# A decoder layer on one core: feed-forwards in blocks of eight width tiles with sums in DRAM, memory keys and values first

## The chip, the core and the metric

One core of a Trainium2 chip runs the whole program. Its engines work side by side and wait for each other by semaphores: PE (TensorE, products), DVE (VectorE), ACT (ScalarE), POOL (GpSimd) and SP (SyncE, which here issues loads). PEld is PE's weight load, which overlaps its products. The metric is the device time of one execution, in microseconds.

## The reference, cut to what matters

All arrays are float32. x is 256 x 2048, mem is 256 x 2048, the width of a feed-forward is 5504 = 43 tiles of 128.

```python
h = swiglu(rms_norm(x, ffn1_pre), ffn1_wg, ffn1_wu, ffn1_wd)   # (silu(u @ wg) * (u @ wu)) @ wd
x = x + 0.5 * rms_norm(h, ffn1_post)
m = hybrid_mixer(rms_norm(x, mix_pre), mem, ...)
x = x + rms_norm(m, mix_post)
h = swiglu(rms_norm(x, ffn2_pre), ffn2_wg, ffn2_wu, ffn2_wd)
x = x + 0.5 * rms_norm(h, ffn2_post)
```

The mixer projects u with w_in (5894 columns) into three branches: a gated linear recurrence (six heads, written hgrn), an attention with a forget gate (six heads, fox) and an attention over the memory (four heads), whose keys and values are rms_norm(mem) @ w_mem_kv (1024 columns). Each branch goes through its own output matrix, is multiplied with a sigmoid gate (u @ w_gate, 6144 columns) and added; w_o closes the mixer.

## The kernel before, in words

**Products.** Every large product goes through `linear` (L249). Its left side lies transposed in SBUF, 128 rows of the contraction (a k tile) by 128 tokens; there are two token tiles t. Both sides are kept as two halves, hi (rounded to the float32r format) and lo (what is left), and one product is three matmuls: hi x hi (L278), hi x lo (L279), lo x hi (L281). The right side comes in column chunks of up to 512, mostly two at a time. `linear` walks k in batches: `head` k tiles first, then two at a time, `tail` last, and in each batch token tile 0 then 1. With `by_chunk` the last batch goes chunk by chunk. `evac` takes the sums out of PSUM and may return a step to be done one batch later (transposes, mostly). `before(k)` is called ahead of a batch, `ahead()` once all weights are asked for.

**Weights** (class at L186). `load` (L204) takes a `raw` tile of 2048 columns, so 1 MB (two k tiles of 1024 columns) per DMA on SP's queue (L217); there are three raw tiles. `split` (L162) makes hi on ACT (L164) and lo on DVE (L165) into rings of N_SPLIT = 6 tiles, one k tile of 1024 columns each. With `early`, the first k tiles go to work tiles instead. The first product of feed-forward 1 loads 512 KB at a time (kb=1).

**Buffers.** 21 work tiles (`slot`, 4 KB per partition), 7 temporaries (`tmp`, 2 KB), 3 raw tiles, PSUM as 5 banks for sums (`acc`) and 3 for transposes (`tp`). The transposed, split input u of a sub-layer has its own tiles (`new_uT`). The order of instructions on each engine is fixed ahead of the run by the framework's scheduler, which takes the program's order as priority and lets a later instruction pass where an earlier one isn't ready; so the constants of L544 to L546 are loaded at the very start.

**Stages.**
1. `before_first` (L484): during the first gate product of feed-forward 1, each chunk of x (128 x 512) is loaded on SP's queue (L464), transposed on PE (L171), multiplied with the gain per row and split (L182 on ACT, L183 on DVE), and its squares are summed (L160 on ACT). The norm's row factor r isn't applied to u: it is given as `scale` when sums leave PSUM (L391, L396).
2. `ffn` (L378): the width goes in three parts, PARTS = (0, 16), (16, 32), (32, 43). In each part gate and up products of 8 width tiles alternate (the last 3 tiles in one product), then the down product over the part, in two halves of 1024 columns. The sums of part 1 are copied to y tiles in SBUF by ACT (L438), part 2 is added by DVE (L440), part 3 is added in the closing step.
3. `closer` (L311): `chunk` adds, sums squares and multiplies with the gain row; `post(t)` makes the row factor (`rsqrt`, L129), adds the residual (L360), stores x (L367) and makes the next sub-layer's transposed input. `begin` issues the gain and residual loads on POOL's queue (L308, L327).
4. During the last down product of feed-forward 1 (`before_close`) and in `before_kv`, memory is prepared as x was. The K/V product follows feed-forward 1 and lies between it and the mixer.
5. Mixer: `proj` products in the order mq, hgrn half 0, hgrn half 1, fox. The recurrences and attentions are generators in `tasks`; `step` runs one step of the first two tasks after each batch of a product.
6. Gates and branches, then w_o with a closing step, whose last batch is BIG = 6 k tiles; the first two weight tiles of feed-forward 2 are split early (`first2`, `ahead`), and its first batch is BIG as well. Then feed-forward 2 and the output, stored by SP (L362).

Of the kernel before, what the change touches and what calls it, by code (L numbers as in the profile page):

```python
# [17 lines left out]
P = 128  # L18
# [35 lines left out]
def layer(ctx: ExitStack, tc: tile.TileContext, a, out: bass.AP):  # L54
# [22 lines left out]

    def acc(w):
        return psp.tile([P, 512], F32, tag="acc", bufs=N_ACC, name=nm("acc"))[:, :w]

    def tp(*shape):
        n = int(np.prod(shape))
        t = psp.tile([P, 512], F32, tag="tp", bufs=N_TP, name=nm("tp"))[:, :n]
        if len(shape) == 2:
            t = t.rearrange("p (a b) -> p a b", b=shape[1])
        return t
# [12 lines left out]
    def columns(rows, q):  # L99
        """Vectors [1, n * 128] as n columns each, found by col()."""  # L100
# [16 lines left out]
    turn_first = columns([("ffn1_pre", 16)], S)  # L117
    turn_rest = columns([("mem_norm", 16), ("mix_pre", 16), ("ffn2_pre", 16), ("hgrn_lb", 12), ("hgrn_gnorm", 6)], G)
# [55 lines left out]
    def split_T(hi, lo, src, n, gain=None):  # L174
        """hi, lo: [P, n, 128] slices for src^T (times gain per row)."""
# [10 lines left out]
    class Weights:  # L186
# [3 lines left out]
        def __init__(self, nk, chunks, kb=None, early=0):  # L190
# [6 lines left out]
            self.kb = kb or max(1, 2048 // self.width)  # L197
# [6 lines left out]
        def load(self, n):  # L204
            width, k0 = self.width, len(self.parts)
            raw = pool.tile([P, 2048], F32, tag="raw", bufs=N_RAW, name=nm("raw"))[:, :n * width]
            raw = raw.rearrange("p (k c) -> p k c", c=width)
# [11 lines left out]
            kh = max(1, 1024 // width)  # L219
            for j in range(0, n, kh):  # L220
                m = min(kh, n - j)
                if k0 + j < self.early:
                    hi, lo = slot([P, 1024], F32R, "ehi"), slot([P, 1024], F32R, "elo")
                else:
                    hi = pool.tile([P, 1024], F32R, tag="whi", bufs=N_SPLIT, name=nm("whi"))
                    lo = pool.tile([P, 1024], F32R, tag="wlo", bufs=N_SPLIT, name=nm("wlo"))
                hi = hi[:, :m * width].rearrange("p (k c) -> p k c", c=width)
                lo = lo[:, :m * width].rearrange("p (k c) -> p k c", c=width)
                split(hi, lo, raw[:, j:j + m, :])
                for i in range(m):  # L230
                    self.parts.append((hi[:, i, :], lo[:, i, :]))
# [717 lines left out]
```

## Time and profile before

| | us |
|---|---|
| median of 3 runs | 2263.7 (2262.32 to 2264.56) |
| span of the profiled execution, first to last instruction | 2262.2 |
| PE busy | 2243.5 |
| DVE busy | 1245.6 |
| ACT busy | 1048.0 |
| POOL busy | 33.1 |

The profile gives the profiled execution's span alone; the runs' times hold also what lies around it. Busy time is the union of an engine's instructions, without those that issue, wait or branch. DMAs moved 434.33 MB, 192 GB/s over the span. The clock granted to PE was 0.998 of full speed in the mean.

### The profile page before, as it was taken

Reading aid. Unit: us, or ns where it says so; the run is one execution under the profiler, and the core shown is the slowest. Engines: PE = TensorE matmul, PEld = TensorE weight load, DVE = VectorE, ACT = ScalarE, POOL = GpSimd, SP = SyncE. Lnnn points to the kernel's source line nnn. Section 1 sums busy time; section 2 is a strip of 40 time slices with the busy share of each in tenths; the row PEclk is TensorE's granted clock in tenths of the full one; section 3 lists DMA queues with packets and bytes.
Section 4 is the critical chain, followed back from the end, with each engine's and each line's share of the span. In section 5 each row is a group of like instructions: output and inputs, shape, how many; then the busy total and the mean of one; then the engine's idle time right before and its main releaser. Section 6 shows DMA issues by size and latency. Waiting matters only on the chain.

```text
span 2262.2 us, 26732 instructions
## 1 busy us (share of the span) xinstructions
PE 2243.5 (99%) x10674; PEld 1914.7 (85%) x10674; DVE 1245.6 (55%) x1519; ACT 1048.0 (46%) x1351; POOL 33.1 (1%) x61
## 2 busy tenths in 40 slices
PE   9999999999999999999999999999999999999998
PEld 7888888888898799999888888888888888888896
DVE  5545445454456856686555545557545445455455
ACT  6444444443446744445444444446444444443443
POOL 0000000000000000000000000000000000000000
PEclk9999999999999999999999999999999999999999
DMA  8555565557555644546656566665656555557553
GB/s 267 187 191 189 178 206 187 201 172 258 188 182 197 224 154 154 166 151 176 194 179 199 187 197 216 217 208 188 203 187 186 187 202 186 186 192 255 179 184 121
DMA packets 138540, 434.33 MB, mean 192 GB/s; under 512 B 9080, under 2 KB 42064, under 8 KB 138416
## 3 DMA queue, kind: packets, MB, share of 16 engines
q1 hardware_dynamic: 133568, 417.41, 55.6%
q0 software_dynamic: 4672, 15.15, 2.4%
q8 instruction: 83, 1.36, 0.2%
q14 instruction: 41, 0.34, 0.0%
q10 hardware_dynamic: 176, 0.07, 0.0%
HBM read 426.30 MB, written 6.30 MB: 191 GB/s over the span
## 4 chain that ended last, share of the span: by engine, by line
PE 97%; DMA 1%; DVE 1%; ACT 0%; SPq 0%; issue 0%; DVEq 0%; ACTq 0%
PE acc L278 31%; PE acc L279 31%; PE acc L281 31%; PE tp L171 2%; PE tp L671 1%; DMA x<-in_x_dram 0%; DMA raw<-in_ffn_wu_dram 0%; DMA x<-in_mem_dram 0%; DVE y L360 0%; DVE wlo L165 0%; ACT whi L164 0%; PE tp L584 0%; PE tp L600 0%; ACT junk L160 0%; PE tp L665 0%; PE tp L818 0%
## 5 line engine op out<-in xcount | busy, mean ns | idle before, releaser
L165 DVE TENSOR_TENSOR wlo<-raw,whi 128x1024 fp32r<-128x1024 f32 (+2 forms) x818 | 958.5, 1177 | 866.0 <-ACT whi L164 829.1
L164 ACT ACTIVATE whi<-raw 128x1024 fp32r<-128x1024 f32 (+2 forms) x818 | 833.2, 1024 | 1006.6 <-PE acc L281 956.4
L278 PE MATMUL acc<-whi,uh 128*128 128x512 f32 (+1 forms) x2264 | 856.6, 379 | 1.6 <-ACT uh L182 1.5
L279 PE MATMUL acc<-wlo,uh 128*128 128x512 f32 (+1 forms) x2264 | 849.2, 376 | 0.8 <-DVE wlo L165 0.8
L281 PE MATMUL acc<-whi,ul 128*128 128x512 f32 (+1 forms) x2264 | 670.2, 376 | 0.1
L278 PEld LDWEIGHTS acc<-whi,uh 128*128 128x128 f32 x2264 | 425.0, 188 | 68.2 <-ACT uh L182 3.0
L279 PEld LDWEIGHTS acc<-wlo,uh 128*128 128x128 f32 x2264 | 425.2, 188 | 66.5 <-DVE wlo L165 1.3
L281 PEld LDWEIGHTS acc<-whi,ul 128*128 128x128 f32 x2264 | 421.1, 188 | 66.6 <-DVE ul L183 0.5
L278 PE MATMUL acc<-whi,hh 128*128 128x512 f32 x688 | 269.2, 391 | 0.0
L279 PE MATMUL acc<-wlo,hh 128*128 128x512 f32 x688 | 268.0, 390 | 0.0
L281 PE MATMUL acc<-whi,hl 128*128 128x512 f32 x688 | 228.4, 389 | 0.0
L281 PEld LDWEIGHTS acc<-whi,hl 128*128 128x128 f32 x688 | 129.1, 188 | 26.9
L278 PEld LDWEIGHTS acc<-whi,hh 128*128 128x128 f32 x688 | 129.2, 188 | 26.5
L279 PEld LDWEIGHTS acc<-wlo,hh 128*128 128x128 f32 x688 | 129.2, 188 | 26.3
L396 DVE SCALAR_TENSOR_TENSOR sg<-acc,rstd,sg 128x512 f32<-128x512 f32 (+1 forms) x44 | 31.2, 733 | 34.3 <-PE acc L281 29.9
L278 PE MATMUL acc<-whi,eh 128*128 128x512 f32 x128 | 50.1, 391 | 0.0
L279 PE MATMUL acc<-wlo,eh 128*128 128x512 f32 x128 | 49.8, 389 | 0.0
L391 ACT ACTIVATE sg<-acc,rstd 128x512 f32<-128x512 f32 (+1 forms) x44 | 27.7, 677 | 44.0 <-PE acc L281 43.3
L281 PE MATMUL acc<-whi,el 128*128 128x512 f32 x128 | 42.9, 391 | 0.0
L183 DVE SCALAR_TENSOR_TENSOR ul<-tp,vec,uh 128x128 fp32r<-128x128 f32 x96 | 29.6, 345 | 7.3 <-ACT uh L182 7.0
L182 ACT ACTIVATE uh<-tp,vec 128x128 fp32r<-128x128 f32 x96 | 31.1, 380 | 5.5 <-DVE ul L183 4.2
L281 PEld LDWEIGHTS acc<-whi,el 128*128 128x128 f32 x128 | 24.0, 188 | 5.0
(262 smaller groups left out, 1097.1 us busy)
## 6 DMA issues: line engine op xcount, KB each, us to landing
raw<-in_ffn_wd_dram SPq DMA_DIRECT2D x84, 1024.0 KB, 5.4
raw<-in_ffn_wu_dram SPq DMA_DIRECT2D x80, 1024.0 KB, 4.9
raw<-in_ffn_wg_dram SPq DMA_DIRECT2D x72, 1024.0 KB, 4.9
raw<-in_w_gate_dram SPq DMA_DIRECT2D x48, 1024.0 KB, 5.2
raw<-in_w_in_dram SPq DMA_DIRECT2D x96, 384.0 KB, 3.7
raw<-in_w_o_dram SPq DMA_DIRECT2D x16, 1024.0 KB, 5.6
raw<-in_ffn_wg_dram SPq DMA_DIRECT2D x16, 512.0 KB, 4.7
raw<-in_w_mem_kv_dram SPq DMA_DIRECT2D x8, 1024.0 KB, 5.0
```

The source lines that it names most:

```text
L164: S.activation(hi, src, AF.Copy)
L165: V.tensor_tensor(lo, src, f32(hi), ALU.subtract)
L171: PE.transpose(p[:, i, :], src[:, i * P:(i + 1) * P], ident)
L182: S.activation(hi[:, i, :], p[:, i, :], AF.Copy, scale=g)
L183: V.scalar_tensor_tensor(lo[:, i, :], p[:, i, :], g, f32(hi[:, i, :]), ALU.mult, ALU.subtract)
L278: PE.matmul(ps[t][c], lh, wh[:, sl], start=(k == 0), stop=False)
L279: PE.matmul(ps[t][c], lh, wl[:, sl], start=False, stop=False)
L281: PE.matmul(ps[t][c], ll, wh[:, span[c]], start=False, stop=(k == nk - 1))
L391: S.activation(sg[t][:, i * 512:i * 512 + p.shape[-1]], p, AF.Silu, scale=r(t))
L396: V.scalar_tensor_tensor(h, p, r(t), h, ALU.mult, ALU.mult)
L671: PE.matmul(L[:, 2 * i + j, :], K[:, i, j * P:(j + 1) * P], Q[:, i, j * 64:(j + 1) * 64], start=True, stop=True)
```

## The change

Sizes: N_SLOT 21 to 28 (the u tiles now come from these), N_TMP 7 to 5, N_RAW 3 of 2048 columns to 8 of 1024, one pool of 8 PSUM banks for `acc` and `tp`. Order: the K/V product is the program's first; in it memory is prepared at k = 0, 4, 8, 12, and x is loaded by POOL (two tiles of 512 KB per token tile, at k = 4 and 10), its rows are summed and multiplied with their row factor (6, 12), transposed and split (8, 14), so that feed-forward 1 needs no row factor. Feed-forwards: after the gate product of each block of 8 width tiles the down product of the block before, whose sums leave PSUM through ACT and are stored or added in DRAM by a DMA of POOL's queue; the last down product (11 width tiles) closes, with the sums loaded back. Closing steps after the first keep the residual times a power of two per row. The first mixer product is hgrn's and has a first batch of BIG; mq follows it.

```diff
-N_SLOT = 21
-N_TMP = 7
-N_RAW = 3
+N_SLOT = 28
+N_TMP = 5
+N_RAW = 8
-N_ACC = 5
-N_TP = 3
+N_BANK = 8
+BLOCK = 8
...
 class Weights:
-            self.kb = kb or max(1, 2048 // self.width)
+            self.kb = max(1, 1024 // self.width)
...
     def new_uT():
...
+        return [[(slot([P, 8, P], F32R, "uh"), slot([P, 8, P], F32R, "ul")) for _ in range(2)] for _ in range(2)]
...
     def closer(y, gpost, factor, resid, keep, gname, final, ms=None, unscale=None):
         def begin(half):
+            if ms is not None:
+                j = slot([P, 1024], F32, "junk")
+                S.activation(j, gp[half], AF.Square, accum_out=g2[:, half:half + 1])
...
+                for t in range(2):
+                    k = scales[t][0] if ms is not None else unscale[t] if unscale is not None else None
+                    if k is not None:
+                        for x in xr[t]:
+                            S.activation(x, x, AF.Copy, scale=k)
...
     def ffn(u, r, first, head, wg, wu, wd, gpost, resid, keep, gname, final, unscale=None):
+        ysum = dram.tile([T, D], F32, name=nm("ysum"))
...
+        def down(f0, f1, close=None):
...
+                    x = tmp([P, 512], "part")
+                    S.activation(x, ps, AF.Copy)
+                    dst = ysum[t * P:(t + 1) * P, c * 512:(c + 1) * 512]
+                    if f0 == 0:
+                        G.dma_start(out=dst, in_=x)
+                    else:
+                        G.dma_start(out=dst, in_=x, accum_op=ALU.add)
...
+                       tail=BIG if close and half else 4, by_chunk=by_chunk)
+        last = n_tile // BLOCK * BLOCK
+        for f in range(0, last, BLOCK):
+            if f == 0:
+                linear(lu, first, gate_plain, head=head)
+            else:
+                linear(lu, Weights(KD, chunks(wg, f, BLOCK)), gate_plain)
+                down(f - BLOCK, f)
+            linear(lu, Weights(KD, chunks(wu, f, BLOCK)), lambda t, ps, f=f: up(t, ps, f, BLOCK))
...
+        def start(half):
+            for t in range(2):
+                G.dma_start(out=y[t][half], in_=ysum[t * P:(t + 1) * P, half * 1024:(half + 1) * 1024])
+            begin(half)
+
+        down(last - BLOCK, n_tile, (start, chunk, post))
...
+    def before_kv(k):
...
+        t = 0 if k < 10 else 1
+        if k in (4, 10):
+            xs[t] = [slot([P, 1024], F32, "xs") for _ in range(2)]
+            for h in range(2):
+                G.dma_start(out=xs[t][h], in_=x_in[t * P:(t + 1) * P, h * 1024:(h + 1) * 1024])
+        if k in (6, 12):
...
+            for c in range(4):
+                sumsq(xs[t][c // 2][:, (c % 2) * 512:(c % 2) * 512 + 512], s_x[t][:, c:c + 1])
+            r = pre_rstd(s_x[t])
+            for h in range(2):
+                S.activation(xs[t][h], xs[t][h], AF.Copy, scale=r)
+        if k in (8, 14):
+            for c in range(4):
+                split_T(*uT_part(u0, t, c), xs[t][c // 2][:, (c % 2) * 512:(c % 2) * 512 + 512], 4, col("ffn1_pre", 4 * c, 4))
...
-           Weights(KD, [(W["w_mem_kv"], 0, 512), (W["w_mem_kv"], 512, 512)]), evac_kv, before=before_kv)
+           Weights(KD, [(W["w_mem_kv"], 0, 512), (W["w_mem_kv"], 512, 512)]), evac_kv, before=before_kv, tail=2)
+    first = Weights(KD, [(W["ffn1_wg"], 0, 512), (W["ffn1_wg"], 512, 512)])
+    u1, st1, sq1 = ffn(u0, None, first, 2, W["ffn1_wg"], W["ffn1_wu"], W["ffn1_wd"], a["ffn1_post"], x_in, x1,
+                       "mix_pre", None)
...
-        proj([(c0, W3), (768 + c0, W3)], evac_qf)
+        proj([(c0, W3), (768 + c0, W3)], evac_qf, head=2 if half else BIG)
...
+    tasks.append(hgrn(0, *hgrn_in(0)))
     proj([(5382, 512)], evac_mq)
     tasks.append(mem_attention())
-    tasks.append(hgrn(0, *hgrn_in(0)))
```

## Rows read from the trace of the kernel before

**Rows 1.** The page, part 1: busy us, share of the span, instructions, by engine.
```profile
PE 2243.5 (99%) x10674; PEld 1914.7 (85%) x10674; DVE 1245.6 (55%) x1519; ACT 1048.0 (46%) x1351; POOL 33.1 (1%) x61
```
**Rows 2.** Stretches: us, busy PE, PEld, DVE, ACT, POOL (instructions), PEclk, DMA share, GB/s.
```profile
0.00:60.00 60.00, 54.50 (x246) 43.64 (x247) 35.45 (x69) 40.86 (x77) 4.48 (x12) 1.00 0.76 252
10.00:20.00 10.00, 9.08 (x42) 7.45 (x42) 7.26 (x12) 7.83 (x17) 0.00 (x0) 1.00 0.87 289
...
730.00:760.00 30.00, 30.00 (x147) 24.60 (x146) 28.93 (x65) 25.48 (x60) 4.34 (x8) 1.00 0.66 229
760.00:790.00 30.00, 28.40 (x135) 23.09 (x135) 22.51 (x65) 21.58 (x46) 0.00 (x0) 1.00 0.60 192
...
950.00:1000.00 50.00, 50.00 (x319) 49.78 (x318) 41.50 (x70) 22.17 (x33) 0.00 (x0) 1.00 0.44 143
...
1490.00:1570.00 80.00, 79.97 (x368) 65.83 (x367) 56.50 (x101) 48.88 (x95) 4.34 (x8) 1.00 0.62 211
...
2245.00:2262.20 17.20, 6.16 (x28) 4.76 (x26) 10.58 (x21) 3.39 (x8) 3.49 (x2) 0.78 0.33 122
```
**Rows 3.** Waits of PE: us in total, times, longest.
```profile
PE tp L171 <- DMA x<-in_x_dram: 1.8, 3, 0.9
PE tp L171 <- DMA x<-in_mem_dram: 1.6, 1, 1.6
...
PE acc L279 <- DVE wlo L165: 0.8, 1, 0.8
```
**Rows 4.** The chain in order of time: start, us, what; transposes of feed-forward 1.
```profile
103.17 0.87 PE tp L171 x8
...
192.03 0.87 PE tp L171 x8
```
**Rows 5.** Groups by line: count, busy us, mean ns, idle before.
```profile
L440 DVE TENSOR_TENSOR y<-acc,y 128x512 f32<-128x512 f32 x16 | 11.0, 690 | 17.8 <-PE acc L281 17.8
...
L438 ACT ACTIVATE y<-acc 128x512 f32<-128x512 f32 x16 | 9.5, 592 | 23.6 <-PE acc L281 23.6
```
**Rows 6.** DMA issues: count, KB each, median us from issue to landing.
```profile
raw<-in_ffn_wg_dram SPq DMA_DIRECT2D x72, 1024.0 KB, 4.9
...
raw<-in_ffn_wg_dram SPq DMA_DIRECT2D x16, 512.0 KB, 4.7
...
x<-in_x_dram SPq DMA_DIRECT2D x8, 256.0 KB, 5.3
```
**Rows 7.** The chain in order of time, its first 50 us: two DMAs.
```profile
2.60 8.42 DMA x<-in_x_dram
...
38.81 7.40 DMA raw<-in_ffn_wu_dram
```
**Rows 8.** Timeline of the start: start us, us, engine, line, operation.
```profile
3.91 0.59 POOL L544 DMA_DIRECT2D causal<-in_c_causal_dram  x1
...
7.42 0.73 PE L278 MATMUL acc<-whi,uh 128*128 128x512 f32 x2 [0.46 <-ACT uh L182]
```
**Rows 9.** ACT's groups by line in the first 60 us.
```profile
L164 ACT ACTIVATE whi<-raw 128x1024 fp32r<-128x1024 f32 x21 | 22.0, 1058 | 11.4 <-DMA raw<-in_ffn_wg_dram 5.9 <-DMA raw<-in_ffn_wu_dram 3.4 <-PE acc L281 1.0
L182 ACT ACTIVATE uh<-tp,vec 128x128 fp32r<-128x128 f32 x32 | 10.3, 360 | 4.3 <-DVE ul L183 3.0 <-PE tp L171 1.3
L160 ACT ACTIVATE junk<-x 128x512 f32<-128x512 f32 x8 | 5.0, 625 | 0.3 <-DMA x<-in_x_dram 0.3
```
**Rows 10.** Timeline of PE, then of DVE, from mixer to feed-forward 2.
```profile
1536.74 0.39 PE L278 MATMUL acc<-ehi,uh 128*128 128x512 f32 x1
...
1549.04 0.47 PE L278 MATMUL acc<-ehi,uh 128*128 128x512 f32 x1
...
1545.32 1.21 DVE L165 TENSOR_TENSOR wlo<-raw,whi 128x1024 fp32r<-128x1024 f32 x1
```
**Rows 11.** Timeline of PE in a mixer product of two chunks of 384.
```profile
868.46 0.33 PE L278 MATMUL acc<-whi,uh 128*128 128x384 f32 x1
...
869.50 0.33 PE L278 MATMUL acc<-whi,uh 128*128 128x384 f32 x1
```

More of the change, by code (lines that the diff above doesn't have):

```diff
@@ L205, in load @@
             width, k0 = self.width, len(self.parts)
-            raw = pool.tile([P, 2048], F32, tag="raw", bufs=N_RAW, name=nm("raw"))[:, :n * width]
-            raw = raw.rearrange("p (k c) -> p k c", c=width)
+            raw = raw_tile()[:, :n * width].rearrange("p (k c) -> p k c", c=width)
             off = 0
@@ L218, in load @@
                 off += w
[L219 to L231, printed above, removed]
+            if k0 < self.early:
+                hi, lo = slot([P, 1024], F32R, "ehi"), slot([P, 1024], F32R, "elo")
+            else:
+                hi, lo = split_tiles()
+            hi = hi[:, :n * width].rearrange("p (k c) -> p k c", c=width)
+            lo = lo[:, :n * width].rearrange("p (k c) -> p k c", c=width)
+            split(hi, lo, raw)
+            for i in range(n):
+                self.parts.append((hi[:, i, :], lo[:, i, :]))
     soon = []
@@ new lines, in post, with ffn, scale, chunks @@
+                q = rsqrt(s3, D) if ms is None else rsqrt(s3, D, 1, scales[t][1])
+                rstd[t] = keep_small()
+                V.tensor_copy(rstd[t], q)
+                V.tensor_scalar(s3, s3, 1.0 / D, None, ALU.mult)
+                square[t] = s3
+        square = {}
+        return begin, chunk, post, lambda: u, rstd, square, scales
+    def ffn(u, r, first, head, wg, wu, wd, gpost, resid, keep, gname, final, unscale=None):
+        hT = {}
+        sg = {}
+        n_tile = DFF // P
+        lu = from_uT(u)
+        ysum = dram.tile([T, D], F32, name=nm("ysum"))
+        if r is not None:
+            minus = [keep_small() for _ in range(2)]
+            for t in range(2):
+                V.tensor_scalar(minus[t], r[t], -1.0, None, ALU.mult)
+        def scale(t, sign=1):
+            return float(sign) if r is None else r[t] if sign > 0 else minus[t]
+        def chunks(W, f, n):
+            return [(W, c * P, min(512, (f + n - c) * P)) for c in range(f, f + n, 4)]
+        def gate_plain(t, ps):
+            sg[t] = slot([P, 1024], F32, "sg")
+            for i, p in enumerate(ps):
+                S.activation(sg[t][:, i * 512:i * 512 + p.shape[-1]], p, AF.Silu, scale=scale(t))
+        def up(t, ps, f, n):
+            g = sg[t]
+            for i, p in enumerate(ps):
+                h = g[:, i * 512:i * 512 + p.shape[-1]]
+                V.scalar_tensor_tensor(h, p, scale(t), h, ALU.mult, ALU.mult)
+            def later():
+                for i in range(0, n, 4):
+                    m = min(4, n - i)
+                    if t == 0:
+                        hT[f + i] = (slot([P, 4, 2, P], F32R, "hh"), slot([P, 4, 2, P], F32R, "hl"))
+                    hh, hl = hT[f + i]
+                    split_T(hh[:, :m, t, :], hl[:, :m, t, :], g[:, i * P:(i + m) * P], m)
+            return later
+        def down(f0, f1, close=None):
@@ L442, in evac2 @@
[L442 to L446 removed]
+                    if close:
+                        close[1](t, c, ps, True)
+                        return
+                    x = tmp([P, 512], "part")
[3 more added lines that the diff above has]
+                        G.dma_start(out=dst, in_=x)
+                    else:
+                        G.dma_start(out=dst, in_=x, accum_op=ALU.add)
@@ L447, in ffn, with evac @@
+                def evac(t, ps, half=half):
+                    if close and half == 1:
+                        close[2](t)
                 rows = wd[f0 * P:f1 * P]
                 wts = Weights(f1 - f0, [(rows, half * 1024, 512), (rows, half * 1024 + 512, 512)])
-                linear(lambda k, t: tuple(h[:, k % 4, t, :] for h in hT[f0 + k - k % 4]), wts, evac2,
-                       tail=BIG if closing and not before_close else 4, by_chunk=by_chunk,
-                       before=before_close if closing else None)
@@ new lines, in both @@
+        def both(t, ps):
+            gate_plain(t, ps[:1])
+            return up(t, ps[1:], last, n_tile - last)
+        linear(lu, Weights(KD, chunks(wg, last, n_tile - last) + chunks(wu, last, n_tile - last)), both)
+        y = [[slot([P, 1024], F32, "y") for _ in range(2)] for _ in range(2)]
+        begin, chunk, post, un, rn, sq, _ = closer(y, gpost, 0.5, resid, keep, gname, final, None, unscale)
+        def start(half):
+            for t in range(2):
+                G.dma_start(out=y[t][half], in_=ysum[t * P:(t + 1) * P, half * 1024:(half + 1) * 1024])
+            begin(half)
@@ L470, in pre_rstd @@
         V.tensor_reduce(s3, s2, AX.X, ALU.add)
-        r = pool.tile([P, 1], F32, tag="rstd", bufs=16, name=nm("rstd"))
+        r = keep_small()
         V.tensor_copy(r, rsqrt(s3, D))
         return r
-    s_x = [small([P, 4], "ss2") for _ in range(2)]
-    r0 = {}
-    u0 = new_uT()
     wp = tp(P)
```

183 lines of the change are left out of this document (67 added, 116 removed).

## The prediction

> **What bounds the kernel now.** I read the page's busy shares first, then the stretches by engine, then PE's waits, then the chain. PE (TensorE) is busy 2243.5 of 2262.2 us [rows 1], so all its idle time is 18.7 us. The stretches say where it lies [rows 2]: 5.5 us in the first 60 us, 1.6 us in 760 to 790 (memory K/V, after feed-forward 1), 11.0 us behind the last product, 0.03 us around the change from mixer to feed-forward 2. That is 18.1 of 18.7 us. The waits name them: x chunks by DMA 1.8 us, a memory chunk 1.6 us, a split weight 0.8 us [rows 3].
>
> A busy PE need not be a PE at its pace, so I check the pace. Two equal points of one block of feed-forward 1, the transposes at 103.17 and 192.03, lie 88.86 us apart [rows 4]. Between them are a gate and an up product (each 16 width tiles x 2 token tiles x 2 chunks x 3 = 192 products of 512 columns) and 16 transposes at 0.87 / 8 = 0.109 us: (88.86 - 1.74) / 384 = 0.227 us. The Trainium skill (Trainium Kernel Development and Optimization, section Performance Expectations) warns that matmul busy time is a bad metric and that weight-load busy share is a good one; here that share is 85% [rows 1], which would leave 15% to win. The change issues the same products with the same operands, so it would leave that share as it is.
>
> The point to see: **the change removes no product and no transpose.** Its kernel can win only idle time, and of that the 11.0 us at the end stay (the last closing chain has the same steps). At most some 7 us are to be had, and every new wait on PE is paid in full.
>
> **The change, part by part.** The sum is made against the profiled span, 2262.2 us. The three runs shown have a median of 2263.7, so 1.5 us lie around the span, and I add them at the end.
>
> *Blocks of 8 and sums in DRAM.* Per feed-forward, down products of 16, 16 and 11 width tiles become four of 8 and one of 11: the same products. The first two down parts had 8 ACT copies at 0.592 us and 8 DVE additions at 0.690 us [rows 5]; now 32 ACT copies, 14 us more ACT and 5.5 us less DVE, and ACT is busy 46% of the span [rows 1]. POOL issues 32 stores or adds of 256 KB, and the sums come back in four loads. An add must wait for the previous one at its place, a block earlier, 88.9 us of gate and up and 192 x 0.227 = 43.6 us of down, so I see no wait. Behind these on POOL stand gain rows and residual rows, issued far ahead of their use. Cost 0; what hides it is the load buffer: 8 tiles of 512 KB are 8 x 12 x 0.227 = 21.8 us of products. Should adds hold up loads longer than that, or the work tiles run out, PE would stop once per block.
>
> *512 KB loads.* SP issues twice as many. The first 16 loads of wg already have this size and land in 4.7 us, the 1 MB ones in 4.9 [rows 6]. PE needs 512 KB per 2.72 us, so two in flight are enough and eight can be. What is gained: a 7.40 us load of wu at 38.81 ended the chain's early stall [rows 7], seen as the 0.8 us wait for a split weight [rows 3]. A deeper ring takes that away: **-0.8 us** (bounds 0 and -0.8).
>
> The Trainium skill (DMA: Bandwidth & Descriptors, section Bandwidth) speaks against this edit: batch loads to 1 MiB or more for at least 75% of peak. What that would do here is the fourth rival.
>
> *Memory K/V first, x loaded and scaled inside it.* Before, x went through PE, ACT and DVE during the first gate product; now memory does in the K/V product, and x follows in the same product. Three terms.
>
> (a) The x rows, four loads of 512 KB, are issued by POOL into free work tiles. POOL has nothing else then: it issued the causal constant at 3.91 us although feed-forward 1 needs it nowhere [rows 8]. So the x loads will go out at about 4 us, among the first weights and memory chunks, while PE's first product starts at 7.42 [rows 8] and the DMA engines are 0.87 busy at 289 GB/s [rows 2]. Upper bound: all their bytes come first, 2.1 MB / 289 GB/s = 7.3 us. Lower bound 0: they fill gaps. Nearest row: an early x chunk took 8.42 us among other loads [rows 7] against a median of 5.3 [rows 6], so I take the difference, **+3.1 us**. The Trainium skill (DMA: Bandwidth & Descriptors, section Issuing engines are not separate DMA queues) says that DMAs of different issuers run on the same 16 engines and interleave; no run here shows x on POOL's queue.
>
> (b) ACT in this product: 16 weight splits at 1.058 us = 16.9, two times 32 transposed tiles = 20.6, 16 sums of squares = 10.0, four row scalings like a weight split = 4.2 [rows 9], K/V copies 4 x 0.592 = 2.4: 54 us. PE: 192 x 0.227 + 64 x 0.109 = 50.6 us. ACT no longer has slack. The bounds are 0 and 3.4 us. Nearest is 730 to 760, where DVE was busy 28.93 of 30 us and PE all 30 [rows 2]; so I stay near the low end, **+1 us**, since the next gate product can take late x tiles of token tile 0 first.
>
> (c) The memory chunk's late load at 760 is gone: **-1.6 us** [rows 3], bounds 0 and -1.6.
>
> *Feed-forward 1 straight into the mixer.* This is the largest term. Before, the K/V product lay between the two and hid the closing chain (sums of squares, root, residual, transposes, splits of token tile 1). Now the first mixer product wants that input at once. The trace has the same crossing at mixer to feed-forward 2 [rows 10]: its first product of token tile 0 starts at 1536.74, that of tile 1 at 1549.04, 12.3 us later, because DVE puts weight splits (the last at 1545.32) between the closing steps. PE lost nothing since it had eight width tiles of token tile 0 to do, two split early into work tiles and six in the ring: 8 x 6 x 0.227 = 10.9 us, and transposes of tile 1, some 12 of its 16 at 0.109, 1.3 us. The new crossing has no early tiles: six width tiles, at two chunks of 384. Six such products take 1.04 us [rows 11], so 6.3 us, and 1.3 of transposes: 7.6. The wait: 12.3, less six splits that are a quarter narrower (6 x 0.31 = 1.8), plus one addition of 0.69 [rows 5] on the path: 11.2. Difference **+3.6 us**. Bounds: 0 (DVE takes the closing steps first) and 9.9 (no weight is split in time, and transposes alone cover). I take the middle value since its mechanism has a measured twin.
>
> *Rows scaled, power-of-two residuals, 28 slots and 5 work buffers.* The squares of the gain rows and the four residual scalings (about 6 us of ACT) stand 30 us ahead of their use. The u tiles take 8 of the 28 slots, so the mixer has 20 for 21, and 5 temporaries for 7. In the mixer DVE is busy 41.5 of 50 us and PE all 50 [rows 2]; eight shared PSUM banks loosen what the temporaries tighten. I take 0, bounds -0.6 (all idle time left over) and +8 (below).
>
> Sum: -0.8 + 3.1 + 1 - 1.6 + 3.6 = +5.3 us. 2262.2 + 5.3 + 1.5 = **2269 us**, +0.23%. Ends of the likely case, by its bounds taken part way: 2264 to 2276.
>
> **Rivals.**
> 1. *All is covered* (2260 to 2265). The static order gives x loads and closing steps good places: terms (a) and the crossing fall to 0, the gains of 2.4 us stay, 2261.3. For: the crossing into feed-forward 2 lost 0.03 us [rows 2]. Against: no early tiles at the new one.
> 2. *Faster*, 2252 to 2259: in place of new stalls the shared banks and the deeper ring also clear the start. Its mechanism is PE taking x and memory transposes from eight banks where it had three; 5.5 + 1.6 us [rows 2] less about 1 us gives 2257.6. It decides only if loads in the first 20 us are not late; 0.87 busy DMA [rows 2] speaks against.
> 3. *Temporaries run dry in the mixer*, 2276 to 2290. Recurrence and attention hold tiles over several steps; a step waiting for a buffer stops DVE with the weight splits behind it. It decides when DVE, 83% busy [rows 2], falls six width tiles behind. Six such stops of 2 us give 2281.
> 4. *Loads become the pace.* If only one were in flight, 512 KB in 4.7 us [rows 6] against 2.72 needed, PE would run at 58%: some 3900 us. A tenth of that loss is still 2430. The sixteen loads of that size did not stop PE [rows 6, 3], hence a small chance. The Trainium skill's rule of 1 MiB, named above, points this way.
>
> **Numbers.** This kernel's runs can tell 0.2%, 4.5 us: faster is below 2259.2, slower above 2268.2. Likely case 0.50, rival 1 0.24, rival 2 0.10, rival 3 0.14, rival 4 0.02. The likely case straddles the bound: I put 0.29 of its 0.50 above. Slower 0.29 + 0.14 + 0.02 = 0.45; faster 0.10 + 0.02 of rival 1 = 0.12; same 0.43. Same and slower share most of the chance, so the likely case's own range is 2264 to 2276. The range for 8 in 10 takes in rival 1, the near edge of rival 2 and half of rival 3: 2259 to 2281.
>
> **What would show it.** PE products and transposes as many as before, pace 0.227 us. In the first 70 us more PE idle than 5.5 us, with x loads on POOL at about 4 us and first chunks landing later. A PE gap of some 4 us, waiting for transposed u of token tile 1, 7 us after feed-forward 1 ends. No wait on partial sums; the same 11 us at the end. Wrong if PE's idle time stays under 18 us, if waits on temporaries appear in the mixer, or if the pace between equal points of a block exceeds 88.9 us without down products.

## The result and the profile after

The changed kernel took 2295.7 us (median of 4 runs, 2294.9 to 2296.4), the kernel before 2264.1 in the runs beside it (2262.3 to 2266.2): ratio 1.0138, 95% interval [1.0123, 1.0152]. It is slower, which had the largest chance (0.45), but by 31.6 us where 5 were forecast, and outside the range of 2259 to 2281. The profiled execution took 2295.1 us with a span of 2293.3, so 31.1 us more span than before.

The page's busy times of the kernel after answer to [rows 1]:

```profile
span 2293.3 us, 28302 instructions
PE 2248.6 (98%) x10674; PEld 1921.5 (84%) x10674; DVE 1234.4 (54%) x1525; ACT 1089.0 (47%) x1421; POOL 89.8 (4%) x137
```

PE has the same 10674 instructions and only 5.1 us more busy time. The other 26 us are idle. The waits of PE answer to [rows 3] and name most of them:

```profile
PE tp L174 <- DVE ym L398: 10.3, 1, 10.3
PE tp L174 <- DVE y L398: 10.1, 1, 10.1
PE tp L174 <- DMA x<-in_mem_dram: 6.9, 2, 6.7
PE acc L283 <- ACT mh L185: 3.8, 3, 2.8
```

The first three are waits of a transpose (tp), not of a product: the transposes of the closing step of the mixer (ym) and of feed-forward 1 (y), and those of the first memory chunks. Only the fourth is a product's wait, for a split memory chunk. The timeline of PE behind feed-forward 1 and behind the mixer shows what stood in line behind each of the first two (start, duration, engine, line, operation, idle time before it and its releaser):

```profile
787.21 0.39 PE L286 MATMUL acc<-whi,hl 128*128 128x512 f32 x1
797.70 3.67 PE L174 MATMUL tp<-ident,y 128*128 128x128 f32 x16 [10.10 <-DVE y L398]
801.03 0.67 PE L283 MATMUL acc<-whi,uh 128*128 128x384 f32 x1
801.49 0.52 PE L284 MATMUL acc<-wlo,uh 128*128 128x384 f32 x1
...
1556.53 0.39 PE L286 MATMUL acc<-whi,el 128*128 128x512 f32 x1
1567.25 3.68 PE L174 MATMUL tp<-ident,ym 128*128 128x128 f32 x16 [10.33 <-DVE ym L398]
1570.58 0.71 PE L283 MATMUL acc<-ehi,uh 128*128 128x512 f32 x1
1571.13 0.39 PE L284 MATMUL acc<-elo,uh 128*128 128x512 f32 x1
```

The last closing product is followed at once by all 16 transposes of token tile 1, which can't start before DVE has closed that tile. The next product's work on token tile 0 stands behind them, although the splits of that tile had ended by 791 at the first place, 7 us before the transposes start. The start of the program has the same picture: the transposes of the first memory chunk of token tile 1 wait 6.70 us for their load, and the K/V product's first work on token tile 0 stands behind them:

```profile
13.57 1.11 PE L174 MATMUL tp<-ident,x 128*128 128x128 f32 x4 [6.70 <-DMA x<-in_mem_dram]
```

The second place in the timeline above, at 1556, is the very crossing of [rows 10], where the kernel before did 12.3 us of token tile 0 in between, and PE was idle for 0.03 us.

The stretches show a second price, in the column of the granted clock (us, busy PE, PEld, DVE, ACT, POOL, PEclk, DMA share, GB/s):

```profile
790.00:797.60 7.60, 0.00 (x0) 0.00 (x0) 7.49 (x20) 3.86 (x9) 0.00 (x0) 0.69 0.62 176
797.60:799.60 2.00, 1.90 (x9) 1.90 (x10) 2.00 (x5) 1.92 (x6) 1.42 (x3) 0.50 1.02 377
799.60:801.60 2.00, 2.00 (x11) 2.00 (x10) 1.38 (x7) 2.00 (x9) 0.75 (x2) 0.50 1.09 419
801.60:803.60 2.00, 2.00 (x9) 2.00 (x8) 2.00 (x9) 2.00 (x10) 0.00 (x0) 0.63 0.59 234
803.60:806.00 2.40, 2.40 (x16) 2.40 (x15) 2.31 (x17) 2.22 (x5) 0.00 (x0) 1.00 0.03 10
```

While PE stands still the clock falls, and it stays at 0.50 (1.2 of 2.4 GHz) after PE has started again, to about 803.1. A group of 16 transposes takes 3.67 us there, where 16 at the pace of [rows 4] take 1.74. If half of the 5.5 us from 797.6 to 803.1 is lost, that is 2.8 us on top of the gap (an estimate from the two clocks).

To place all of it, I took PE's starts from the trace, and from each start to the next what lies beyond the usual distance of the same pair of lines. Summed by stage, this is the PE time lost, in us (the numbers of the experiments' kernels stand here too, since they are read against each other). The entries are estimates: another choice of the usual distance moves them by up to 2 us in the first stretch and by 1 or so elsewhere.

| kernel | 0 to 120 | 120 to 690 (feed-forward 1) | 690 to 860 (into the mixer) | 860 to 1500 (mixer) | 1500 to 1600 (into feed-forward 2) |
|---|---|---|---|---|---|
| before | 7.8 | 0.4 | 5.7 | 5.7 | 1.0 |
| after | 16.7 | 0.1 | 14.2 | 7.0 | 13.1 |
| before, one shared pool | 10.0 | 0.3 | 29.3 | 5.4 | 13.0 |
| after, split banks | 12.3 | 0.2 | 5.7 | 12.4 | 1.7 |
| after, closing step moved | 17.6 | 0.1 | 7.7 | 7.7 | 1.3 |
| split banks, x by SP | 10.6 | 0.3 | 5.6 | 12.8 | 1.7 |
| ... and 7 temporaries | 9.6 | 0.3 | 5.6 | 6.8 | 1.6 |
| ... memory earlier | 9.5 | 0.3 | 5.8 | 7.1 | 1.7 |
| ... early width tiles | 9.4 | 0.2 | 3.7 | 7.5 | 1.7 |
| all of these, shared pool, order mended | 14.4 | 0.2 | 4.9 | 6.6 | 1.3 |

Between before and after it places 30.5 of the 31.1 us: 8.9 at the start, 8.5 and 12.1 at the two crossings, 1.3 in the mixer, nothing in the feed-forwards. Behind the last product PE is idle for 10.0 us, 11.0 before, so 1.6 us stay without a place:

```profile
2270.00:2293.30 23.30, 13.29 (x59) 10.68 (x57) 13.35 (x26) 6.62 (x15) 3.49 (x2) 0.88 0.24 90
```

### The profile page after: what moved, and what is told of

The parts are those of the page before. It is cut to its first block, busy times and chain, and to the rows that moved or that the text cites. A ratio compares the mean times of both kernels' runs of the same rounds, so it can differ in the third digit from the quotient of the medians.

```text
span 2293.3 us, 28302 instructions
## 1 busy us (share of the span) xinstructions
PE 2248.6 (98%) x10674; PEld 1921.5 (84%) x10674; DVE 1234.4 (54%) x1525; ACT 1089.0 (47%) x1421; POOL 89.8 (4%) x137
## 4 chain that ended last, share of the span: by engine, by line
PE 95%; ACT 2%; DVE 1%; DMA 1%; issue 1%; SPq 0%; DVEq 0%; POOL 0%; ACTq 0%; POOLq 0%
PE acc L283 31%; PE acc L284 30%; PE acc L286 30%; PE tp L174 2%; PE tp L723 1%; ACT junk L163 1%; DMA x<-in_mem_dram 0%; ACT whi L167 0%; DVE wlo L168 0%; ACT uh L185 0%; DVE y L398 0%; DMA B<-cbuf 0%; PE tp L652 0%; PE tp L636 0%; ACT xs L562 0%
## 5 line engine op out<-in xcount | busy, mean ns | idle before, releaser
L167 ACT ACTIVATE whi<-raw 128x1024 fp32r<-128x1024 f32 (+2 forms) x818 | 830.8, 1024 | 920.8 <-PE acc L286 874.9
L286 PE MATMUL acc<-whi,hl 128*128 128x512 f32 x688 | 239.2, 389 | 0.0
L283 PEld LDWEIGHTS acc<-whi,hh 128*128 128x128 f32 x688 | 129.2, 188 | 26.7
L468 ACT ACTIVATE part<-acc 128x512 f32<-128x512 f32 x64 | 37.9, 592 | 94.4 <-PE acc L286 94.4
L473 POOL DMA_DIRECT2D ysum<-part x48 | 41.6, 866 | 753.3 <-ACT part L468 647.9
L283 PE MATMUL acc<-whi,mh 128*128 128x512 f32 x64 | 26.3, 411 | 3.8 <-ACT mh L185 3.8
## 6 DMA issues: line engine op xcount, KB each, us to landing
raw<-in_w_mem_kv_dram SPq DMA_DIRECT2D x16, 512.0 KB, 10.1
```

The costliest lines, as they stand in the source:

```text
L283: PE.matmul(ps[t][c], lh, wh[:, sl], start=(k == 0), stop=False)
L286: PE.matmul(ps[t][c], ll, wh[:, span[c]], start=False, stop=(k == nk - 1))
L468: S.activation(x, ps, AF.Copy)
L473: G.dma_start(out=dst, in_=x, accum_op=ALU.add)
```

## The experiments

**Theory.** One pool of eight banks for sums (acc) and transposes (tp) gives its banks in the order in which the program first uses them. The next product's sums are used later in the program than the closing transposes of token tile 1, so PE's instructions are laid out with the transposes ahead. Separate pools (five and three) have no such order between the two. How the framework gives out banks isn't shown here; the runs below show what PE's order follows, not why. **Rivals:** the u tiles moved into the work pool run short; the temporaries run short; the eight banks are simply too few at a crossing, whatever the order.

### 1. Split the banks in the changed kernel; share them in the kernel before

After, with split banks:

```diff
-N_BANK = 8
+N_ACC = 5
+N_TP = 3
...
-        return psp.tile([P, 512], F32, tag="bank", bufs=N_BANK, name=nm("acc"))[:, :w]
+        return psp.tile([P, 512], F32, tag="acc", bufs=N_ACC, name=nm("acc"))[:, :w]
...
-        t = psp.tile([P, 512], F32, tag="bank", bufs=N_BANK, name=nm("tp"))[:, :n]
+        t = psp.tile([P, 512], F32, tag="tp", bufs=N_TP, name=nm("tp"))[:, :n]
```

> The changed kernel with one edit undone: sums get 5 PSUM banks and transposes 3, two pools as before. Theory A, order by the shared bank pool: with one pool a sum tile that stands later in the program gets no bank before an earlier transpose tile has one, so the next product of token tile 0 is put behind the 16 closing transposes of token tile 1, and PE idles 10 us twice (and about 6 us at the start); then this kernel loses both gaps and the half-clock stretch behind each, some 12 + 12 us, and a few us of the start: 2266 to 2272 us, PE idle at the two crossings under 5 us together. Rival B, the closing chain itself has become longer (work tiles for u, extra scalings, no K/V product in between): 2290 us or more, gaps of 10 us stay. Rival C, adds in DRAM or 512 KB loads cost it: 2290 us or more as well.

Measured: 2276.0 us (2275.5 to 2277.3), ratio to before 1.0053 [1.0037, 1.0070]. 19.6 of the 31.6 us are gone, with both gaps; the losses at the crossings are 5.7 and 1.7 us for 14.2 and 13.1. The long wait of the start goes too (PE's waits of this kernel):

```profile
PE tp L175 <- DMA x<-in_mem_dram: 1.6, 2, 1.3
```

Twelve products of token tile 0 now run there, from 7.75 to 11.8 us, ahead of the transposes of the second chunk. The time stayed 4 us above what was expected, since a new stop came up in the mixer (experiment 4).

The kernel before, the same edit the other way round:

```diff
-N_ACC = 5
-N_TP = 3
+N_BANK = 8
```

> The kernel before with that one edit done: one pool of 8 PSUM banks for sums and transposes, nothing else. Theory A: the closing transposes of token tile 1 come ahead of the K/V product after feed-forward 1 and ahead of feed-forward 2's first product, so two gaps of some 8 to 11 us appear where the kernel before has none, plus their half-clock stretches and 2 to 5 us at the start: 2284 to 2292 us. Rivals B and C: the edit alone changes nothing, 2262 to 2266 us.

Measured: 2302.5 us (2302.2 to 2302.8), ratio 1.0169 [1.0154, 1.0184]. Sharing alone makes the kernel before 38 us slower. That is 10 us over the upper end of what was expected; a stop was not foreseen, the third of PE's waits in this kernel:

```profile
PE tp L170 <- DVE y L359: 13.1, 1, 13.1
PE tp L170 <- DVE ym L359: 10.3, 1, 10.3
PE tp L170 <- DMA x<-in_mem_dram: 8.3, 1, 8.3
PE tp L170 <- DMA x<-in_x_dram: 4.7, 2, 4.1
```

The 8.3 us are a stop within the last down product, from 701 to 709: a transpose of a memory chunk that hasn't landed holds up products that need nothing of it. Behind it the granted clock is 0.50 up to 714.

### 2. The u tiles in tiles of their own

```diff
-N_SLOT = 28
+N_SLOT = 20
...
-        return [[(slot([P, 8, P], F32R, "uh"), slot([P, 8, P], F32R, "ul")) for _ in range(2)] for _ in range(2)]
+        return [[tuple(pool.tile([P, 8, P], F32R, tag=f"u{t}{j}{x}", bufs=1, name=nm("u" + x)) for x in "hl")
+                 for j in range(2)] for t in range(2)]
```

> The changed kernel with the transposed inputs u in tiles of their own (eight tiles out of the 28 work tiles), the bank pool still shared. Rival B in its form that the work tiles hold up the order: the gaps shrink, 2270 to 2280 us. Theory A: the order on PE stays, 2293 to 2298 us.

Measured: 2294.4 us (2293.9 to 2298.3), ratio 1.0137, as the changed kernel's 1.0138; the waits of 10.3 and 10.1 us stand unchanged. That the u tiles come from the work tiles is not the cause.

### 3. Keep the shared pool, change the place in the program

This is the direct test. Nothing of the pool is changed; the closing step of token tile 1 is put on a list that the next product runs behind its first batch of token tile 0 (the row scales that need that step move with it).

```diff
+                if t == 0 and bi == 0:
+                    while between:
+                        between.pop(0)()
...
-                    if close and half == 1:
-                        close[2](t)
+                    if close and half == 1:
+                        if t == 0 or final is not None:
+                            close[2](t)
+                        else:
+                            between.append(lambda: close[2](1))
...
-            if half == 1:
-                post(t)
+            if half == 1 and t == 0:
+                post(t)
+            elif half == 1:
+                between.append(lambda: post(1))
```

> The changed kernel, its one pool of eight shared banks kept; only the place in the program of the second closing step differs: the closing step of token tile 1 (root, residual, transposes) is now written behind the first batch of token tile 0 of the next product, at both crossings, where it stood ahead of that whole product. Theory (a shared pool gives its banks in the order in which the program first uses them, so the next product's sums had to stand behind the closing transposes): the two PE gaps of 10.3 and 10.1 us fall to under 2 us each with the pool still shared, and with them the half clock behind them: 2295.7 - 8 - 11 = 2276, 2272 to 2281. Rival (eight banks in one pool run out at the crossings, whatever the order): the gaps stay, 2290 to 2297. The start (18 us of PE time lost) stays as it is in both.

Measured: 2277.9 us (2276.7 to 2279.9), ratio 1.0061 [1.0047, 1.0074]: 17.8 us back with the pool as it is. The timeline of PE at the first crossing of this kernel:

```profile
788.00 0.39 PE L287 MATMUL acc<-whi,hl 128*128 128x512 f32 x1
789.19 0.62 PE L284 MATMUL acc<-whi,uh 128*128 128x384 f32 x2 [0.81 <-ACT whi L167]
791.35 1.01 PE L285 MATMUL acc<-wlo,uh 128*128 128x384 f32 x2 [1.54 <-DVE wlo L168]
...
798.64 0.51 PE L287 MATMUL acc<-whi,ul 128*128 128x384 f32 x2
799.11 2.12 PE L174 MATMUL tp<-ident,y 128*128 128x128 f32 x12
```

Thirty-six products of token tile 0 now stand ahead of the transposes, and of these only the last four wait, 0.4 us. What is left are two short stops for weight splits. So it is the order and not the number of banks, and the rival of too few banks falls. The start, whose order was not touched, keeps its loss (17.6 us), and its wait for the memory chunk (5.5 us).

### 4. What split banks leave: temporaries

With split banks a stop of 3.5 us stands in the mixer. PE's wait, then DVE and POOL around it (rows of the waits, and the timelines of DVE and of POOL, of the changed kernel with split banks):

```profile
PE tp L175 <- DVE fqT L848: 3.5, 1, 3.5
```

```profile
1055.84 0.95 DVE L169 TENSOR_TENSOR wlo<-raw,whi 128x768 fp32r<-128x768 f32 x1
1062.00 0.42 DVE L865 TENSOR_TENSOR B<-B,causal 128x256 f32<-128x256 f32 x1 [5.22 <-DMA B<-cbuf]
...
1063.21 0.55 DVE L848 COPY fqT<-tp 128x384 f32<-128x384 f32 x1
```

```profile
1055.30 0.56 POOL L862 DMA_DIRECT2D B<-cbuf  x1 [22.49 <-PE tp L175]
1055.85 0.54 POOL L863 DMA_DIRECT2D B<-cbuf  x1
```

DVE waits in its order for the bias tile B, whose load POOL issued only at 1055.30, after 22.5 us of waiting for a transpose to release a temporary; the copy fqT, on which PE waits, stands behind it. Three runs on this. First x loaded by SP, which the next ones are built on (it belongs to the start, experiment 5), then 7 temporaries:

```diff
-N_SLOT = 28
-N_TMP = 5
+N_SLOT = 27
+N_TMP = 7
```

> The run with split banks and x loaded by SP (2273.7 us), with 7 temporaries for 5 and 27 work tiles for 28. Theory (the gap of 3.7 us in the mixer and other mixer losses, 11.6 us against 3.8 before, come from temporaries that run dry, as the prediction's third rival had it): the mixer loses 4 to 6 us, 2266 to 2269. Rival (the mixer's new order of the products, memory queries behind the recurrence's inputs, makes it): no change, 2272 to 2276.

Measured: 2268.5 us (2267.7 to 2269.9), ratio 1.0019 [1.0010, 1.0028], against 2273.7 and 1.0042 without it: 5.1 us back, the mixer's loss falls from 12.8 to 6.8. The load of B now goes out 15 us earlier than in the row above, and 13 earlier than with x by SP alone (1053.64):

```profile
1040.30 0.56 POOL L862 DMA_DIRECT2D B<-cbuf  x1 [10.21 <-DVE sm L138]
```

The rival, the mixer's new order of products:

```diff
-        proj([(c0, W3), (768 + c0, W3)], evac_qf, head=2 if half else BIG)
+        proj([(c0, W3), (768 + c0, W3)], evac_qf, head=2)
...
-    tasks.append(hgrn(0, *hgrn_in(0)))
-    proj([(5382, 512)], evac_mq)
+    proj([(5382, 512)], evac_mq, head=BIG)
     tasks.append(mem_attention())
+    tasks.append(hgrn(0, *hgrn_in(0)))
```

> The run with split banks and x loaded by SP (2273.7 us), with the mixer's first products in the order of the kernel before: memory queries first, then the inputs of the first half of the recurrence. Theory (temporaries): no change, 2271 to 2276. Rival (order): the mixer loses 4 to 6 us for 11.6, 2266 to 2269. It may also cost at the crossing, as the first product has one chunk of 512 and so covers 6 x 3 x 0.227 = 4.1 us where two chunks of 384 cover 6.3: up to 2.2 us on top in both.

Measured: 2276.3 us (2273.4 to 2277.7), ratio 1.0051 [1.0037, 1.0065]; the wait for fqT is still there (3.9 us). That is 0.3 us over the range for temporaries and 7 over the one for the order. The order is not the cause. And the temporaries alone, in the kernel before (N_TMP 5 for 7):

> The kernel before with 5 temporaries for 7, nothing else. Theory (five temporaries are short for the mixer by themselves): 3 to 7 us slower, 2267 to 2271, the loss between 1000 and 1150 us. Rival (five are short only together with the changed order of the products and the u tiles among the work tiles): 2263 to 2265.

Measured: 2270.0 us (2268.0 to 2271.4), ratio 1.0023 [1.0014, 1.0032]: 5.6 us, with the same stop (POOL's idle time before the load of B is 22.49 us here too):

```profile
PE tp L171 <- DVE fqT L795: 3.8, 1, 3.8
```

The changed kernel itself has the same late load, as POOL's timeline shows, but no stop of PE comes of it; why is not shown:

```profile
1068.10 0.56 POOL L861 DMA_DIRECT2D B<-cbuf  x1 [22.43 <-PE tp L174]
```

### 5. What split banks leave: the start and the first crossing

x loaded by SP, in its order among the weights, for POOL (banks split):

```diff
-                G.dma_start(out=xs[t][h], in_=x_in[t * P:(t + 1) * P, h * 1024:(h + 1) * 1024])
+                nc.sync.dma_start(out=xs[t][h], in_=x_in[t * P:(t + 1) * P, h * 1024:(h + 1) * 1024])
```

> The first kernel of this call (two bank pools) with the four early x loads issued by SP among the weights, not by POOL at 6 to 9 us. Theory: x loads of POOL take DMA time from the first weights and memory chunks, so moving them gains 2 to 5 us against the kernel with two bank pools, seen before 40 us. Rival: the deeper ring of weight loads ahead of the memory chunks holds up the start, and x plays no part: within 1 us of it.

Measured: 2273.7 us (2272.2 to 2275.7), ratio 1.0042 [1.0027, 1.0057] against 1.0053 [1.0037, 1.0070]. The medians differ by 2.4 us, but the intervals overlap; the table has 1.7 us less lost at the start. The two kernels' stretches say why it isn't more (split banks with x by POOL, then x by SP):

```profile
10.00:20.00 10.00, 7.98 (x36) 5.75 (x34) 6.28 (x10) 5.49 (x10) 0.00 (x0) 1.00 1.03 407
```
```profile
10.00:20.00 10.00, 9.30 (x41) 7.28 (x42) 8.85 (x14) 8.55 (x18) 0.00 (x0) 1.00 1.03 405
```

Both move 405 to 407 GB/s at a DMA share of 1.03. What changed is when x is asked for: its first load is issued at 6.60 us by POOL and at 14.36 by SP. The Trainium skill (DMA: Bandwidth & Descriptors, section Issuing engines are not separate DMA queues) says that DMAs of different issuers run on the same 16 engines and interleave; the nearly equal rates of these two rows agree.

Then, on top of 7 temporaries, memory chunks 1 to 3 one batch earlier:

```diff
-        if k % 4 == 0:
-            c = k // 4
+        for c in [0] if k == 0 else [(k + 2) // 4] if k % 4 == 2 and k < 14 else []:
```

> The run with split banks, x loaded by SP and 7 temporaries (2268.5 us), with memory chunks 1 to 3 loaded, transposed and split one batch (two width tiles) earlier in the K/V product. There PE still stops 2.5 us at 33.5 us for the split of a memory chunk by ACT. Theory (ACT, with x's squares, scalings and splits and the weight splits, comes late with that chunk; the prediction's term b): the stop goes, -1.5 to -2.5 us, 2266 to 2267. Rival (ACT is simply full there, and the stop moves to the next work of ACT): 2268 to 2269.

Measured: 2267.5 us (2267.2 to 2268.0), ratio 1.0014 [1.0005, 1.0023] against 1.0019 [1.0010, 1.0028]. The stop at 33.7 (2.2 us of idle time) is gone, but the loss of the start is 9.5 us for 9.6: other stops came instead, of 1.2 us at 11.6, 0.9 at 42.5, 0.8 at 48 and 0.6 at 50. A gain of 1 us at best, not told from none. The time lies between the two ranges; the stops that moved speak for the rival.

And two width tiles of the mixer's first product split early, into work tiles, as at the other crossing:

```diff
+    mix_first = Weights(KD, [(W["w_in"], 0, W3), (W["w_in"], 768, W3)], early=2)
...
-                       "mix_pre", None)
+                       "mix_pre", None, ahead=lambda: mix_first.need(2))
```

> As the run with memory chunks earlier, and the first two width tiles of the mixer's first product loaded and split into work tiles ahead of feed-forward 1's closing batch, as the crossing into feed-forward 2 has it. There PE still stops 1.1 and 1.6 us at 780 to 784 for weight splits by DVE. Theory (the closing steps on DVE hold the weight splits back): both stops go, another -2.5 us, 2263 to 2265, level with the kernel before. Rival (splits move from one place of a full DVE to another): no change against the run with memory chunks earlier.

Measured: 2265.6 us (2265.4 to 2266.5), ratio 1.0004 [0.9995, 1.0013]: level with the kernel before, and 0.6 us over what was expected. Of the two stops at 781 and 783 (1.0 and 1.5 us of idle time) the first is gone, and 1.2 us of the second stay. With these edits the 31.6 us are given back but for 1.2, which can't be told from none, one part at a time (by the table the start and the mixer still lose 1.6 and 1.8 us more than before, the crossing into the mixer 2.0 less), while feed-forwards in blocks of 8, the sums in DRAM, the 512 KB loads and the moved K/V product are all still in.

### 6. 512 KB loads alone, in the kernel before

```diff
-N_RAW = 3
+N_RAW = 6
...
-            self.kb = kb or max(1, 2048 // self.width)
+            self.kb = max(1, 1024 // self.width)
...
-            raw = pool.tile([P, 2048], F32, tag="raw", bufs=N_RAW, name=nm("raw"))[:, :n * width]
+            raw = pool.tile([P, 1024], F32, tag="raw", bufs=N_RAW, name=nm("raw"))[:, :n * width]
```

> The kernel before with its weights loaded 512 KB at a time, six raw tiles of 4 KB a partition for three of 8; nothing else is changed. Theory (half the size costs nothing, since 512 KB landed in 4.3 to 5.5 us in the changed kernel against 4.9 for 1 MB, and its feed-forwards lose no PE time): 2262 to 2266. Rival (the rule of 1 MiB): the loads are slower per byte, waits for split weights appear in the feed-forwards, over 2269.

Measured: 2265.5 us (2264.3 to 2267.1), ratio 1.0006 [0.9997, 1.0015]. No difference. In its feed-forward 1 PE is busy without a gap:

```profile
120.00:690.00 570.00, 570.00 (x2596) 478.65 (x2595) 280.77 (x256) 242.34 (x256) 3.16 (x6) 1.00 0.62 196
```

The Trainium skill's rule to batch loads to 1 MiB or more for at least 75% of peak (DMA: Bandwidth & Descriptors, section Bandwidth) doesn't bear here: the stage moves 196 GB/s with PE busy throughout, and half the size delivers that.

### 7. All mendings with the shared pool

Eight shared banks, the closing steps and the first memory chunk of token tile 1 written behind the next product's first batch, x by SP, 7 temporaries, memory earlier, early width tiles.

```diff
-            for t in range(2):
-                xc = tmp([P, 512], "x0")
+            def chunk_of(t, c=c):
+                xc = tmp([P, 512], "x0")
...
+            chunk_of(0)
+            if c == 0:
+                between.append(lambda f=chunk_of: f(1))
+            else:
+                chunk_of(1)
```

> All mendings together, but with the one pool of eight shared banks kept: x loaded by SP, 7 temporaries, memory chunks one batch earlier, two early width tiles of the mixer's first product, and the closing step of token tile 1 as well as the first memory chunk of token tile 1 written behind the first batch of token tile 0 of the product that follows. Theory (a shared pool costs only by the order that it imposes; with the program in the wanted order eight banks are as good as five and three, or better): level with the same kernel with split banks (2265.6 us), 2262 to 2266. Rival (sharing has a price of its own, sums and transposes taking each other's banks): 2268 or more. Better than the kernel before beyond doubt only under 2260.

Measured: 2270.4 us (2270.1 to 2271.6), ratio 1.0028 [1.0017, 1.0039]; 4.8 us slower than its twin with split banks. The theory's number was missed, and the time lies in the range of the rival, that sharing has a price of its own. The table puts it at the start, 14.4 us lost for 9.4; the crossings are about as good (4.9 and 1.3 us for 3.7 and 1.7). PE's waits in this kernel are again of transposes that stand ahead of products:

```profile
PE tp L174 <- ACT xs L578: 3.5, 2, 2.5
PE tp L174 <- DVE ul L186: 2.1, 1, 2.1
```

There x's and the memory's later transposes stand in the K/V product in an order that was not mended. So it is likely the same mechanism once more, at places that were left as they were. That is not shown: it was not tried whether moving them too would bring the rest, and until then the rival stands for these 4.8 us. No kernel tried here is faster than the one before.

## Why the prediction was wrong

**The step that failed** is the one that costed the banks at nothing. It said that eight shared PSUM banks loosen what the temporaries tighten, and counted them, in the second rival, as a gain at the start. And it took the crossing of [rows 10] as a pattern for the new kernel, where PE has eight width tiles of token tile 0 to do while DVE closes token tile 1: that this order would stay was never asked. Sharing took it away at both crossings, and put a memory chunk's transposes ahead of ready products at the start. It cost 19.6 us in the changed kernel (split banks) and 17.8 by the order alone (closing step moved), of 26.7 by which the forecast was off. In the kernel before it cost 38 us by itself. Most of what then remains is the temporaries, which the sum also put at nothing: 2276.0 with split banks less the 5.1 us that seven temporaries gave would be 2271 (an estimate; that pair was not run alone), 2 us over the forecast. The other terms thus add up nearly right, in part by luck, since they missed in both directions.

Point by point, by the terms of the sum:

- *The pace.* Right: the same number of PE instructions, and 0.1 to 0.4 us lost in feed-forward 1 in every kernel. *Blocks of 8 and sums in DRAM:* right at 0. No wait of PE on partial sums shows, and POOL's 48 adds of 256 KB (41.6 us busy in all) are covered.
- *512 KB loads.* Right at about 0: the kernel before with them gives 1.0006. The gain of 0.8 us can't be told from none.
- *(a) x among the first loads, +3.1.* Right in kind. The loads went out at 6.65 us, not at 4, and a 512 KB load of the K/V weights then took 10.1 us to land (5.0 for 1 MB of them in the kernel before, where they come later). SP in POOL's place gained 2.4 us by the medians, 1.7 by the trace. But the longest stop of the start was one that the prediction didn't have, the 6.70 us of a memory chunk's transposes.
- *(b) ACT level with PE, +1.* Of the right size as far as it shows: at most 1.0 us came back when memory was moved ahead. The stop itself was 2.2 us long; with it gone, PE waited elsewhere in the same product. What was not counted is a table load of 1.28 us in the row scaling's root, which sits 0.8 us ahead of that stop (ACT's timeline of the kernel with 7 temporaries):

```profile
31.67 1.28 ACT L139 ACT_TABLE_LOAD   x1
```

- *(c) The late memory chunk at 760, -1.6.* Right: that wait is gone there. Memory chunks wait for their loads at the start instead.
- *The crossing into the mixer, +3.6.* Hidden behind the 10.1 us in the changed kernel; with split banks it is two stops of 1.0 and 1.5 us, a little less than forecast, and for another reason: PE waits for weight splits on DVE, not for the transposed u of token tile 1. Early width tiles gave 1.9 us by the medians.
- *Work tiles and residual scaling, 0.* Right for the work tiles by the kernel with u tiles of its own. The scalings had no run of their own; no wait of PE names them.
- *Temporaries, 0 with a bound of +8.* Five are short: 5.6 us in the kernel before, 5.1 with split banks. The third rival had the place and roughly the cause (a tile held over several steps, DVE stopped with weight splits behind it), but it is one stop of 3.8 us by way of a late load on POOL, not six of 2. With shared banks that stop does not show (7.0 us lost in the mixer, 5.7 before), so there the sentence that the banks loosen it held, at a price far above its worth; by what path is not shown.

**The rivals.** "All is covered" and "faster" fall. "Temporaries run dry" is right as a part. "Loads become the pace" falls with the 512 KB run. The case that came was not among them: a static order made by the allocation.

**The signs.** The start lost more than 5.5 us, as listed, and the end 10.0 for the 11 forecast. A gap stood between feed-forward 1 and the mixer, but of 10.1 us for 4, at once and not 7 us later, and on the closing transposes themselves. Of the signs for "wrong" one showed, and off PE: POOL's wait of 22.43 us for a temporary in the mixer. The list lacked the one that mattered, a closing transpose with the whole next product behind it.

## What to carry to other kernels

Before you merge two pools, ask which of their tiles is first used earlier in the program and which of them waits longest: in the one pool of this kernel the later tile stood behind the earlier one, and PE, which took its work in the order laid out, stood behind the slow chain. Here 16 transposes that take under 2 us of work held up the next product for 10 us, twice. If sharing is wanted, write the slow step behind the first work that can cover it. And a buffer count cut in one place (temporaries) may show only once another bound (banks) is taken away, so undo the parts of a change one by one, and in the old kernel too.

## What the runs showed of the hardware that was not expected

- A stop of PE can cost more than its length, and a short one can do so too. Behind the gap of 10.1 us PE ran at 0.50 of its clock for 5.5 us, 2.8 us lost; behind the stop in the mixer of the kernel before with 5 temporaries, with 3.8 us of wait, it ran at half for about 3 us:

```profile
1055.00:1058.80 3.80, 0.37 (x3) 0.04 (x1) 1.48 (x3) 0.37 (x1) 1.06 (x2) 1.00 0.91 248
1058.80:1062.00 3.20, 2.87 (x10) 2.87 (x11) 2.13 (x5) 1.90 (x4) 0.00 (x0) 0.51 0.17 32
```

  Even the two stops of 0.81 and 1.54 us in the kernel with the closing step moved (experiment 3), with two products between them, were followed by 3 us at half the clock, but two stops of 0.97 and 1.45 us at 782 and 784, with six products between them, were not (third row, split banks with x by SP):

```profile
789.00:791.30 2.30, 0.62 (x2) 0.30 (x2) 2.30 (x8) 2.30 (x9) 0.00 (x0) 0.98 0.00 0
791.30:794.30 3.00, 2.95 (x8) 2.58 (x9) 2.92 (x8) 2.98 (x5) 0.00 (x0) 0.50 0.42 131
...
780.00:786.00 6.00, 3.25 (x16) 2.08 (x15) 5.79 (x18) 6.00 (x16) 0.00 (x0) 1.00 0.21 66
```

- With x, weights and memory all asked for at once, the DMA engines of the changed kernel moved 402 to 408 GB/s at a share of 1.02 to 1.03 between 10 and 30 us (x by POOL or by SP made no difference to that). The prediction had taken the 289 GB/s at 0.87 of [rows 2] for near full. What went with it is the landing time: 10.1 us for 512 KB of K/V weights, where loads of that size in its feed-forwards took 4.3 to 5.5. In the first of these rows the clock is 0.60, behind the stop of 6.70 us:

```profile
10.00:20.00 10.00, 6.43 (x21) 5.30 (x22) 5.32 (x10) 5.23 (x10) 0.00 (x0) 0.60 1.02 402
20.00:30.00 10.00, 9.53 (x47) 7.84 (x46) 7.06 (x10) 6.74 (x13) 0.00 (x0) 1.00 1.03 408
```
